# Projection stage: a third modulation group loaded earlier and multiplied inside the second step, and the decay constants moved to another pool

## The chip, the cores and the metric

The program runs on one core of a Trainium2 chip. The metric is the device time of one execution in microseconds (us), as the median of several runs; lower is better.

## The reference, cut to what matters

One layer of a diffusion backbone is applied to 128 context tokens and 512 latent tokens, together five tiles of 128 tokens, with 1024 channels. All is float32. The part that the change touches is the beginning: a modulated RMS norm, whose scale and shift come from a product of the conditioning vector with `w_mod`, and the projection of the result by `w_in`.

```
sh1, sc1, g1, sh2, sc2, g2 = adaln(c, w_mod[l], b_mod[l])       # silu(c) @ w_mod + b_mod, in six parts
h = rmsnorm(xs, norm1_g[l]) * (1.0 + sc1) + sh1
z = h @ w_in                                                    # q, k, v, rq, rk, rv, rg, ga, gr
...
lg_f = jax.nn.log_sigmoid(dec_f.astype(jnp.float32))            # retention: decay per head
q_decay = jnp.exp(lg * (i + 1.0))
k_decay = jnp.exp(lg * (CHUNK - 1.0 - i))
chunk_decay = jnp.exp(log_gamma * CHUNK)
```

The attention branch uses q, k, v; the retention branch uses rq, rk, rv, rg and the decays, which are functions of eight numbers for each direction. Both branches are projected, gated, added, and a gated MLP follows.

## The kernel before

TensorE multiplies in a fast 32-bit type, and each operand is split into a high part (a cast, by ScalarE) and a low part (the difference, by VectorE). One product of the reference thus becomes three matmuls (`mm3`, L158 to L161): high by high, high by low, low by high.

**The first stage** (from L426) is written out by hand, in the order of the instructions on TensorE, VectorE and ScalarE (`manual_schedule`). The tokens are normalised and transposed. Then eight steps follow, one for each block k of 128 channels. Step k, `z_kv(k)`, multiplies block k of all five token tiles by the 512 columns of `w_in` that make k and v, and adds into five PSUM banks `kvb` (mm1.mm.11 to mm1.mm.15). That is 15 matmuls a step. Before step k can start, four things must be there:

- `kv_hi` and `kv_lo` (L319, L324): high and low part of the weights of two steps, out of `weights.raw` (w_in, loaded at L313).
- `mod_mm(g)` (L386): products of the conditioning with the columns of `w_mod` for the channels of group g. The five groups hold 1, 1, 2, 2 and 2 blocks; their tiles are p0.u3 to p0.u7, each loaded by two transfers (L307), the scale's columns and the shift's. Group 2, p0.u5, serves the steps 2 and 3.
- `mod_row(g)` (L394) copies that product to SBUF, and `mod_vec(g)` (L400, a small matmul, then L402 and L404 on VectorE) turns it into vectors. `mod_vec` stands inside a step, after its second tile.
- `mod_hi(k)` (L409 on VectorE, L411 the cast on ScalarE) and `mod_lo(k)` (L414 on VectorE): block k modulated and split.

The loads are issued by SyncE's queue (SP) in the order of the lines from L327 on.

**The second stage** takes the five banks off: for each tile ScalarE copies k (L547) and casts v (L548) and squares k (L555), VectorE takes v's low part (L549) and sums (L556); tile 0 also has a copy (L552). Each bank is then reused: the q projection (`a_group`, five tiles with 12 matmuls for each half of the contraction) writes mm1.mm.16 into the bank of mm1.mm.11. GpSimd builds rotary tables meanwhile (L563, L566). From here on the program's order on each engine is set by a scheduler that places instructions by estimated times and by the buffers that they need; only the marked blocks keep the written order.

**The decay constants** (`decay_consts`, L576 to L599): 32 small operations on VectorE, on at most 16 numbers a row, and three on ScalarE, written after the attention and ahead of the attention's output projection. Their input `dec` and their scratch `dtmp` are tiles of the pool `const`, which is never reused, and so the scheduler could put the loads (L773, L774) and the chain much earlier than they are written. Their results `lg`, `lgsel`, `cdsel`, `kdec` are first used in the retention stage, after the output projection of the attention.

**The attention's output projection** (from L766) splits the attention's result (L645), multiplies it by `w_att_o` (L194 to L196, banks mm3.mm), and takes the banks off by L785 on VectorE; its pool `mod`, on the right side of SBUF, also holds the conditioning (`s128`) and one tile for `w_mod` (mod.wm, L248).

Of the kernel before, what the change touches and what calls it, by code (L numbers as in the profile page):

```python
# [69 lines left out]
def hybrid_step(ctx: ExitStack, tc: tile.TileContext, a: dict, o: dict):  # L70
# [40 lines left out]
    shvec = [cp([P, 8, 2]) for _ in range(2)]  # L111
    dec = cp([P, 2, 8])
    lg = cp([P, 2, 8])
    lgsel = cp([P, 8])
    cdsel = cp([P, 8])
    kdec = cp([P, 8, 2])
    dtmp = [cp([P, 2, 8]) for _ in range(3)]
    sso = cp([P, 2, NT, 4])
# [210 lines left out]
    kv_load(0, 2)  # L329
    mod_load(1)  # L330
    kv_load(2, 2)
    mod_load(2)
# [80 lines left out]
    def mod_lo(k):  # L413
        V.tensor_sub(hT[1][:, k, :], xnT[k // 4][:, k % 4], hT[0][:, k, :].bitcast(F32))  # L414
# [1174 lines left out]
```

## Time and profile before

| what | value |
|---|---|
| three runs | 1191.09, 1191.26 (median), 1192.38 us |
| the profiled execution | 1192.46 us, of which its span (first to last instruction) is 1190.7 us |
| mean granted TensorE clock | 0.994 |
| TensorE busy | 1156.5 us (97% of the span) |
| VectorE, ScalarE, GpSimd busy | 737.5, 567.4, 174.7 us |

All moments in this document are us from the start of the span. A row of the timeline gives the start, the duration, the engine, the line, the operation and the names "out<-in"; a bracket at its end tells how long the engine had been idle and who ended that. PE is TensorE, PEld its weight loads, DVE VectorE, ACT ScalarE, POOL GpSimd, SP SyncE, and a q behind a name is an engine's queue. Matmuls overlap: the next one starts before the one ahead has ended, so that the distance of the starts is what one costs. Lines are those of the kernel before; the changed kernel's stand one or two lower up to the attention and one higher after it.

### The profile page before, as it was taken

The page shows a single profiled execution, that of the slowest core. Times are in us where ns is not written, and L with a number is a line of the kernel's source. Part 1 is how long each engine was busy: PE and PEld are TensorE (multiplying, and loading weights), DVE is VectorE, ACT ScalarE, POOL GpSimd, SP SyncE. Part 2 cuts the span into 40 slices and gives each one's busy share as a digit, 9 for nine tenths or more (in the row PEclk, how much of TensorE's full clock was granted, in tenths as well). Part 3 has the DMA queues.
Part 4 walks back from the last instruction along what each step waited for, and adds up shares of the span by engine and source line. Part 5 has one row for each costly group of instructions (what it writes and reads, how often), then busy time and mean ns, then how long its engine had stood idle before and what let it go on. Part 6 is the DMA issues. An engine that isn't in the chain of part 4 may idle for free.

```text
span 1190.7 us, 18327 instructions
## 1 busy us (share of the span) xinstructions
PE 1156.5 (97%) x7317; PEld 1041.0 (87%) x7317; DVE 737.5 (62%) x1419; ACT 567.4 (48%) x1019; POOL 174.7 (15%) x177
## 2 busy tenths in 40 slices
PE   4999999999999999999999999999999999999996
PEld 3778899999988888778999988998989999899995
DVE  5576777754333526454323338968767687598887
ACT  4345655553132324443322335567657557475473
POOL 0032200000002200043011122011112111121113
PEclk9999999999999999999999999999999999999998
DMA  8831211016544522111122339536666658556553
GB/s 283 269 110 48 71 37 36 3 34 212 199 165 139 185 89 87 37 36 45 62 72 71 135 131 156 135 66 134 159 131 120 142 140 172 129 108 149 141 111 120
DMA packets 130917, 139.02 MB, mean 117 GB/s; under 512 B 26240, under 2 KB 98000, under 8 KB 130832
## 3 DMA queue, kind: packets, MB, share of 16 engines
q1 hardware_dynamic: 106592, 112.95, 29.3%
q0 software_dynamic: 24240, 24.91, 13.8%
q8 instruction: 57, 0.93, 0.3%
q14 instruction: 28, 0.23, 0.1%
HBM read 110.32 MB, written 6.03 MB: 98 GB/s over the span
## 4 chain that ended last, share of the span: by engine, by line
PE 89%; DVE 5%; SPq 1%; ACT 1%; DMA 1%; issue 1%; POOL 1%; DVEq 0%; POOLq 0%; ACTq 0%
DMA p0.u5.5_130<-in_w_mod 1%; SPq L313 0%; SPq L307 0%; POOL f0.s.5_3520 L940 0%; DVE acts.u2.2_101 L1104 0%; PE aux1.aux.6_337 L386 0%; DVE x1.u1.1_6376 L1076 0%; DVE acts.u1.1_100 L1103 0%; PE mm1.mm.16_720 L159 0%; PE mm7.mm.45_9650 L1383 0%; PE mm7.mm.9_7496 L1386 0%; PE mm7.mm.57_10402 L1383 0%; PE mm7.mm.33_8918 L1383 0%; PE mm7.mm.63_10768 L1385 0%; PE mm7.mm.54_10133 L1383 0%
## 5 line engine op out<-in xcount | busy, mean ns | idle before, releaser
L829 POOL TENSOR_TENSOR ret.r2k.6_3630<-ret.u5.5_3523,ret.u1.1_3516 128x256 f32<-128x256 f32 x2 | 1.4, 740 | 205.1 <-ACT ret.u5.5_3523 L825 205.1
L1397 DVE TENSOR_TENSOR t7.u4.4_6925<-t7.u4.4_6925,const.u1.1_70 128x322 f32<-128x322 f32 x10 | 5.0, 495 | 11.7 <-ACT const.u1.1_70 L1396 11.7
L878 DVE SCALAR_TENSOR_TENSOR ret2.u1.1_4317<-ret2.u1.1_4317,const.u14.14_94 64x128 f32<-64x128 f32 x24 | 6.8, 338 | 6.6 <-ACT ret2.u1.1_4317 L871 6.5
L411 ACT CAST acts.u1.1_100<-f0.s.1_113 128x640 fp32r<-128x640 f32 x4 | 2.9, 727 | 16.0 <-DVE f0.s.1_113 L409 16.0
L152 DVE TENSOR_TENSOR weights.wh.183_6565<-weights.raw.181_6562,weights.wh.182_6564 128x1024 fp32r<-128x1024 f32 x1 | 1.2, 1224 | 14.3 <-ACT weights.wh.182_6564 L147 14.3
L1308 POOL TENSOR_TENSOR x1.u1.1_6376<-x1.u1.1_6376,weights.raw.410_10987 128x512 f32<-128x512 f32 x5 | 8.2, 1637 | 10.4 <-ACT x1.tm.112_11000 L1280 7.5
L880 DVE SCALAR_TENSOR_TENSOR ret2.u1.1_4317<-ret2.u1.1_4317,const.u14.14_94 64x128 f32<-64x128 f32 x24 | 6.6, 383 | 4.8 <-ACT ret2.u1.1_4317 L873 4.8
L831 DVE TENSOR_TENSOR ret.u5.5_3523<-ret.u5.5_3523,ret.u1.1_3516 128x512 f32<-128x512 f32 x5 | 3.5, 692 | 9.4 <-POOL ret.r2k.8_3701 L829 3.3
L831 DVE TENSOR_TENSOR ret.u4.4_3522<-ret.u4.4_3522,ret.u1.1_3516 128x512 f32<-128x512 f32 x5 | 3.5, 692 | 9.0 <-POOL ret.r2k.11_3881 L829 4.7
L373 PE MATMUL mm1.mm.1_171<-const.u1.1_70,xin.u1.1_112 128*128 128x128 f32 x4 | 1.1, 432 | 7.1 <-DVE xin.u1.1_112 L364 7.1
L411 ACT CAST acts.u1.1_100<-f0.s.2_114 128x640 fp32r<-128x640 f32 x4 | 2.9, 727 | 10.6 <-DVE f0.s.2_114 L409 10.6
L563 POOL TENSOR_TENSOR p1.u1.1_613<-p1.u3.3_617,p1q.u1.1_607 128x512 f32<-128x512 f32 x1 | 1.4, 1428 | 43.2 <-DMA p1.u3.3_617<-in_rope 43.2
L152 DVE TENSOR_TENSOR weights.wh.108_4347<-weights.raw.106_4344,weights.wh.107_4346 128x1024 fp32r<-128x1024 f32 x1 | 1.2, 1225 | 10.3 <-ACT weights.wh.107_4346 L147 10.3
L147 ACT CAST weights.wh.112_4502<-weights.raw.111_4500 128x1024 fp32r<-128x1024 f32 x1 | 1.1, 1050 | 13.3 <-PE mm3.mm.36_4215 L160 13.3
L940 POOL TENSOR_TENSOR f0.s.5_3520<-f0.s.5_3520,ret2.ny20.11_4899 128x512 f32<-128x512 f32 x5 | 6.0, 1235 | 9.1 <-DVE ret2.ny20.11_4899 L219 9.1
L532 ACT ACTIVATE f0.s.3_719<-f0.s.3_719,p1q.ny20.11_887 128x128 f32<-128x128 f32 x20 | 6.0, 388 | 2.5 <-DVE p1q.ny20.11_887 L217 2.5
L373 PEld LDWEIGHTS mm1.mm.1_171<-const.u1.1_70,xin.u1.1_112 128*128 128x128 f32 x4 | 0.7, 216 | 7.3 <-DVE xin.u1.1_112 L364 7.3
L867 POOL DMA_DIRECT2D out_new_state_ret_fwd<-ret.r2k.25_4340 x1 | 0.7, 670 | 43.8 <-ACT ret.r2k.25_4340 L866 43.8
L259 DVE COPY mod2.wr.9_4307<-aux3.aux.15_4274 128x128 f32<-128x128 f32 x1 | 0.3, 291 | 10.9 <-PE aux3.aux.15_4274 L256 10.9
L1274 DVE TENSOR_TENSOR x1.u1.1_6376<-x1.u1.1_6376,gate.u1.1_5306 128x512 f32<-128x512 f32 x10 | 6.7, 681 | 0.0
L147 ACT CAST weights.wh.182_6564<-weights.raw.181_6562 128x1024 fp32r<-128x1024 f32 x1 | 1.1, 1055 | 11.5 <-PE mm3.mm.83_6396 L160 11.5
L147 ACT CAST weights.wh.67_3356<-weights.raw.66_3354 128x1024 fp32r<-128x1024 f32 x1 | 1.0, 1045 | 11.5 <-PE mm3.mm.8_3138 L195 11.5
(7028 smaller groups left out, 4884.6 us busy)
## 6 DMA issues: line engine op xcount, KB each, us to landing
spill.u1.1_6384<-x1.u1.1_6376 POOLq DMA_DIRECT2D x5, 512.0 KB, 4.2
xin.u1.1_112<-in_x_sample SPq DMA_DIRECT2D x4, 512.0 KB
p0.u5.5_130<-in_w_mod SPq DMA_DIRECT2D x2, 1024.0 KB
p0.u6.6_135<-in_w_mod SPq DMA_DIRECT2D x2, 1024.0 KB
p0.u7.7_138<-in_w_mod SPq DMA_DIRECT2D x2, 1024.0 KB
mod.wm.2_2916<-in_w_mod SPq DMA_DIRECT2D x1, 2048.0 KB
mod.wm.4_3067<-in_w_mod SPq DMA_DIRECT2D x1, 2048.0 KB
mod.wm.6_3222<-in_w_mod SPq DMA_DIRECT2D x1, 2048.0 KB
```

The lines of the kernel that those rows point to most:

```text
L147: nc.scalar.copy(hi, rv)
L152: (lo_eng or V).tensor_sub(lo, rv, hi.bitcast(F32))
L373: nc.tensor.transpose(xps[t, g][:, j * P:(j + 1) * P], xin[:, t, k * P:(k + 1) * P], ident)
L411: nc.scalar.copy(hT[0][:, k, :], xk)
L532: nc.scalar.activation(x[:, j], x[:, j], AF.Copy, scale=rstd[:, j:j + 1])
L831: V.tensor_mul(z, z, r1[:, t, 0:1, :].to_broadcast([P, 8, 64]))
L878: V.scalar_tensor_tensor(Ss[0:64, hh, st + 1, j], Ss[0:64, hh, st, j], cdsel[0:64, h:h + 1], Ss[0:64, hh, st + 1, j], op0=ALU.mult, op1=AL ...
L880: V.scalar_tensor_tensor(Ss[64:128, hh, 2 - st, j], Ss[64:128, hh, 3 - st, j], cdsel[64:128, h:h + 1], Ss[64:128, hh, 2 - st, j], op0=ALU. ...
L940: nc.gpsimd.tensor_mul(ov, ov, rso[:, 4 * t:4 * t + 4].unsqueeze(2).to_broadcast([P, 4, P]))
L1274: V.tensor_mul(x1[:, t, gs], x1[:, t, gs], gb[:, t == 0, gs])
L1308: eng.tensor_mul(x, x, fg[:, c0:c0 + 512])
L1397: V.tensor_sub(u[1][:, hi_u], u[1][:, hi_u], u3[i])
```

## The change

It has two parts that do not touch each other in the code.

1. `dec` and `dtmp` are no longer tiles of the pool `const` but of the pool `mod`, which is opened after the attention, on memory that the attention's buffers had.
2. In the first stage, the loads of group 2 of `w_mod` are issued ahead of the load of the weights of the steps 2 and 3. `mod_mm(2)`, with its `mod_row`, stands no longer ahead of step 1 but inside it, after its second tile, and `mod_vec(2)` after its third. `kv_lo(2)` stands behind `mod_hi(2)`, and `kv_lo(6)` behind `mod_lo(6)`, no longer ahead of `mod_mm(4)`.

```
-    dec = cp([P, 2, 8])
-    dtmp = [cp([P, 2, 8]) for _ in range(3)]
...
     mod_load(1)
+    mod_load(2)
     kv_load(2, 2)
-    mod_load(2)
...
-    def z_kv(k, mid=None):
+    def z_kv(k, mid=None, first=None):
         wh, wl = (x[:, (k % 2) * 512:(k % 2) * 512 + 512] for x in wkv[k - k % 2][1:])
         for t in range(NT):
             ts = slice(t * P, (t + 1) * P)
             mm3(kvb[t], hT[0][:, k, ts], hT[1][:, k, ts], wh, wl, k == 0, k == KD - 1)
-            if mid is not None and t == 1:
+            if first is not None and t == 1:
+                mod_mm(first)
+            if mid is not None and t == (1 if first is None else 2):
                 mod_vec(mid)
...
         kv_hi(2)
+        z_kv(1, 2, 2)
+        mod_hi(2)
         kv_lo(2)
-        mod_mm(2)
-        z_kv(1, 2)
-        mod_hi(2)
         mod_lo(2)
...
         kv_hi(6)
-        kv_lo(6)
         mod_mm(4)
         z_kv(4, 4)
         mod_hi(6)
         mod_lo(6)
+        kv_lo(6)
...
     mp = Pool("mod", side="right")
+    dec = mp([P, 2, 8])
+    dtmp = [mp([P, 2, 8]) for _ in range(3)]
     nc.sync.dma_start(dec[:, 0, :], a["decay_fwd"][0:1, :].to_broadcast([P, 8]))
     nc.sync.dma_start(dec[:, 1, :], a["decay_bwd"][0:1, :].to_broadcast([P, 8]))
-    decay_consts()
+    decay_consts(dec, dtmp)
```

The order of the instructions changes at these places. First SyncE's queue near the program's start, before the change, where p0.u4, p0.u5 and p0.u6 are the groups 1, 2 and 3 of `w_mod`, weights.raw.1 (its second half) the weights of the steps 2 and 3, and weights.raw.2 those of the steps 4 to 7:

```order
L307 DMA p0.u4.4_126<-in_w_mod 128x8x128 x2
L313 DMA weights.raw.1_124<-in_w_in 128x2x512
L307 DMA p0.u5.5_130<-in_w_mod 128x8x256 x2
L313 DMA weights.raw.2_133<-in_w_in 128x4x512
L307 DMA p0.u6.6_135<-in_w_mod 128x8x256 x2
```

And the same place after it:

```order
L305 DMA p0.u4.4_122<-in_w_mod 128x8x128 x2
L305 DMA p0.u5.5_125<-in_w_mod 128x8x256 x2
L311 DMA weights.raw.1_120<-in_w_in 128x2x512
L311 DMA weights.raw.2_129<-in_w_in 128x4x512
L305 DMA p0.u6.6_131<-in_w_mod 128x8x256 x2
```

The two transfers of group 2 (x2 in their row) went past one transfer of weights. On TensorE, at the end of step 0 and the beginning of step 1, before the change (the banks mm1.mm.11 to mm1.mm.15 are the five tiles of a step, aux1.aux.6 takes `mod_mm(2)`):

```order
L161 MATMUL mm1.mm.15_308<-weights.wh.3_241,acts.u2.2_101 128x512
L386 MATMUL aux1.aux.6_337<-p0.u5.5_130,p0.s128.8_146 32x128 x32
L159 MATMUL mm1.mm.11_304<-weights.wh.3_241,acts.u1.1_100 128x512
L160 MATMUL mm1.mm.11_304<-weights.wh.4_242,acts.u1.1_100 128x512
L161 MATMUL mm1.mm.11_304<-weights.wh.3_241,acts.u2.2_101 128x512
L159 MATMUL mm1.mm.12_305<-weights.wh.3_241,acts.u1.1_100 128x512
L160 MATMUL mm1.mm.12_305<-weights.wh.4_242,acts.u1.1_100 128x512
L161 MATMUL mm1.mm.12_305<-weights.wh.3_241,acts.u2.2_101 128x512
L400 MATMUL aux1.aux.7_378<-const.u1.1_70,p0.mrow.24_370 128x8
```

And after it:

```order
L159 MATMUL mm1.mm.15_304<-weights.wh.3_237,acts.u2.2_97 128x512
L157 MATMUL mm1.mm.11_300<-weights.wh.3_237,acts.u1.1_96 128x512
L158 MATMUL mm1.mm.11_300<-weights.wh.4_238,acts.u1.1_96 128x512
L159 MATMUL mm1.mm.11_300<-weights.wh.3_237,acts.u2.2_97 128x512
L157 MATMUL mm1.mm.12_301<-weights.wh.3_237,acts.u1.1_96 128x512
L158 MATMUL mm1.mm.12_301<-weights.wh.4_238,acts.u1.1_96 128x512
L159 MATMUL mm1.mm.12_301<-weights.wh.3_237,acts.u2.2_97 128x512
L384 MATMUL aux1.aux.6_338<-p0.u5.5_125,p0.s128.8_142 32x128 x32
L157 MATMUL mm1.mm.13_302<-weights.wh.3_237,acts.u1.1_96 128x512
L158 MATMUL mm1.mm.13_302<-weights.wh.4_238,acts.u1.1_96 128x512
L159 MATMUL mm1.mm.13_302<-weights.wh.3_237,acts.u2.2_97 128x512
L398 MATMUL aux1.aux.7_376<-const.u1.1_70,p0.mrow.24_371 128x8
```

The 32 products of group 2 now follow six matmuls of step 1 that they stood ahead of. On VectorE, at the steps 4 and 5, before the change (p0.mrow.26 is the row of group 4, weights.wh.10 the low part of the weights of the steps 6 and 7, and the first row is `mod_lo(5)`):

```order
L414 TENSOR_TENSOR acts.u2.2_101<-f0.s.2_114,acts.u1.1_100 128x640
L324 TENSOR_TENSOR weights.wh.10_481<-weights.raw.2_133,weights.wh.9_480 128x1024
L394 COPY p0.mrow.26_517<-aux1.aux.10_484 128x128
L402 TENSOR_TENSOR p0.u1.1_111<-aux1.aux.11_525,const.u3.3_83 128x2x4
L404 TENSOR_TENSOR p0.u1.1_111<-p0.u1.1_111,const.u3.3_83 128x4
```

And after it:

```order
L412 TENSOR_TENSOR acts.u2.2_97<-f0.s.2_110,acts.u1.1_96 128x640
L392 COPY p0.mrow.26_512<-aux1.aux.10_479 128x128
L400 TENSOR_TENSOR p0.u1.1_107<-aux1.aux.11_520,const.u3.3_83 128x2x4
L402 TENSOR_TENSOR p0.u1.1_107<-p0.u1.1_107,const.u3.3_83 128x4
L407 TENSOR_SCALAR f0.s.2_110<-f0.s.2_110,p0.u1.1_107 128x512
L407 TENSOR_SCALAR f0.s.2_110<-f0.s.2_110,p0.u1.1_107 128x128
L412 TENSOR_TENSOR acts.u2.2_97<-f0.s.2_110,acts.u1.1_96 128x640
L322 TENSOR_TENSOR weights.wh.10_477<-weights.raw.2_129,weights.wh.9_476 128x1024
```

The split of the weights went behind the row's copy and behind block 6. Last, VectorE where the banks are taken off, before the change (kv.u4 is v's low part, const.u16 and const.u18 the decays' scratch; ahead of these rows stand, since the split weights.wh.18, thirteen more operations of L581 to L588):

```order
L574 TENSOR_TENSOR kv.u4.4_603<-p1.vc.6_622,kv.u3.3_602 128x256
L587 TENSOR_TENSOR const.u16.16_96<-const.u16.16_96,const.u18.18_98 128x16
L588 TENSOR_SCALAR const.u16.16_96<-const.u16.16_96 128x16
L549 TENSOR_TENSOR kv.u4.4_603<-mm1.mm.11_304,kv.u3.3_602 128x256
L552 COPY p1.vt.7_627<-mm1.mm.11_304 128x256
```

And after it:

```order
L150 TENSOR_TENSOR weights.wh.15_728<-weights.raw.11_721,weights.wh.14_727 128x1024
L412 TENSOR_TENSOR acts.u2.2_97<-f0.s.2_110,acts.u1.1_96 128x640
L150 TENSOR_TENSOR weights.wh.18_794<-weights.raw.16_791,weights.wh.17_793 128x1024
L548 TENSOR_TENSOR kv.u4.4_599<-mm1.mm.11_300,kv.u3.3_598 128x256
L551 COPY p1.vt.7_623<-mm1.mm.11_300 128x256
```

No operation of the decays stands between the split of the weights and the banks any more. All of `decay_consts` now stands on VectorE in the attention's output projection: the first operation (L578), which waits for the load of `dec`, behind the third of the eight splits L645, the others among the first four L785. On SyncE the two loads of `dec` stand ahead of the first load of mod.wm, and they wait for three instructions near the attention's end: the transposition into aux2.aux.50 (TensorE), and L699 (ScalarE) and L702 (VectorE) of the last context block. Of the other 6115 rows of TensorE only some at the beginning of the output projection change places among themselves.

More of the change, by code (lines that the diff above doesn't have):

```diff
@@ L111, in hybrid_step @@
     shvec = [cp([P, 8, 2]) for _ in range(2)]
-    dec = cp([P, 2, 8])
     lg = cp([P, 2, 8])
@@ L116, in hybrid_step @@
     kdec = cp([P, 8, 2])
-    dtmp = [cp([P, 2, 8]) for _ in range(3)]
     sso = cp([P, 2, NT, 4])
@@ L330, in hybrid_step @@
     mod_load(1)
+    mod_load(2)
     kv_load(2, 2)
-    mod_load(2)
     kv_load(4, 4)
@@ L414, in mod_lo, with z_kv @@
         V.tensor_sub(hT[1][:, k, :], xnT[k // 4][:, k % 4], hT[0][:, k, :].bitcast(F32))
-    def z_kv(k, mid=None):
+    def z_kv(k, mid=None, first=None):
         wh, wl = (x[:, (k % 2) * 512:(k % 2) * 512 + 512] for x in wkv[k - k % 2][1:])
@@ L420, in z_kv @@
             mm3(kvb[t], hT[0][:, k, ts], hT[1][:, k, ts], wh, wl, k == 0, k == KD - 1)
-            if mid is not None and t == 1:
+            if first is not None and t == 1:
+                mod_mm(first)
+            if mid is not None and t == (1 if first is None else 2):
                 mod_vec(mid)
@@ L478, in hybrid_step @@
         kv_hi(2)
+        z_kv(1, 2, 2)
+        mod_hi(2)
         kv_lo(2)
-        mod_mm(2)
-        z_kv(1, 2)
-        mod_hi(2)
         mod_lo(2)
@@ L495, in hybrid_step @@
         kv_hi(6)
-        kv_lo(6)
         mod_mm(4)
@@ L500, in hybrid_step @@
         mod_lo(6)
+        kv_lo(6)
         mod_hi(7)
@@ L574, in hybrid_step, with decay_consts @@
     V.tensor_sub(vv[1][:, 5, :], vc.rearrange("p h d -> p (h d)"), vv[0][:, 5, :].bitcast(F32))
-    def decay_consts():
+    def decay_consts(dec, dtmp):
         e, s, s2 = dtmp
@@ L772, in hybrid_step @@
     mp = Pool("mod", side="right")
+    dec = mp([P, 2, 8])
+    dtmp = [mp([P, 2, 8]) for _ in range(3)]
     nc.sync.dma_start(dec[:, 0, :], a["decay_fwd"][0:1, :].to_broadcast([P, 8]))
     nc.sync.dma_start(dec[:, 1, :], a["decay_bwd"][0:1, :].to_broadcast([P, 8]))
-    decay_consts()
+    decay_consts(dec, dtmp)
     ada = mod_rest((("sc", 1, 4096), ("sh", 1, 3072)), mp, aux)
```

## The prediction

> **What bounds the kernel now.** I read the totals first, then who waited for whom, then windows of 2 us, then the timeline of the first 75 us.
>
> ```profile
> PE 1156.5 (97%) x7317; PEld 1041.0 (87%) x7317; DVE 737.5 (62%) x1419; ACT 567.4 (48%) x1019; POOL 174.7 (15%) x177
> ...
> PE mm1.mm.16_720 L159 <- DVE p1.vt.7_627 L552: 2.9, 1, 2.9
> PE aux1.aux.6_337 L386 <- DMA p0.u5.5_130<-in_w_mod: 2.3, 1, 2.3
> PE aux1.aux.11_525 L400 <- DVE p0.mrow.26_517 L394: 1.1, 1, 1.1
> ```
>
> TensorE is the bound: 97% busy, with few waits. Three of these (who waited, for whom, total, times, longest) lie where the change works. TensorE also slows after the longer ones. A row of the windows gives the stretch, its length, the busy time (and instructions) of PE, PEld, DVE, ACT and POOL, then the granted clock PEclk, the DMA share and GB/s:
>
> ```profile
> 28.00:30.00 2.00, 0.27 (x4) 0.00 (x0) 2.00 (x3) 0.67 (x1) 0.00 (x0) 1.00 1.07 372
> 30.00:32.00 2.00, 1.43 (x28) 1.34 (x32) 0.32 (x1) 0.00 (x0) 0.00 (x0) 0.61 1.05 377
> 32.00:34.00 2.00, 2.00 (x40) 1.59 (x32) 0.00 (x0) 0.00 (x0) 0.00 (x0) 0.53 1.09 348
> ...
> 50.00:52.00 2.00, 1.28 (x6) 0.71 (x4) 1.87 (x2) 1.85 (x2) 0.00 (x0) 1.00 0.00 0
> ...
> 68.00:70.00 2.00, 1.69 (x4) 1.43 (x5) 2.00 (x7) 1.41 (x6) 0.93 (x1) 0.50 0.03 10
> ```
>
> Behind the waits of 2.3 and 2.9 us the clock is near half; at the wait of 1.1 us, which begins at 51.3, it is 1.00. So each long wait is paid twice.
>
> **Term 1: group 2 inside step 1.** On TensorE, and on the engines that feed step 2:
>
> ```profile
> 27.53 0.40 PE L161 MATMUL mm1.mm.15_308<-weights.wh.3_241,acts.u2.2_101 128*128 128x512 f32 x1
> ...
> 28.50 0.68 DVE L324 TENSOR_TENSOR weights.wh.4_242<-weights.raw.1_124,weights.wh.3_241 128x512 fp32r<-128x512 f32 x1
> ...
> 29.10 1.22 DVE L324 TENSOR_TENSOR weights.wh.6_334<-weights.raw.1_124,weights.wh.5_333 128x1024 fp32r<-128x1024 f32 x1
> ...
> 30.57 3.53 PE L386 MATMUL aux1.aux.6_337<-p0.u5.5_130,p0.s128.8_146 128*32 128x128 f32 x60 [2.30 <-DMA p0.u5.5_130<-in_w_mod]
> ...
> 35.52 0.28 PE L400 MATMUL aux1.aux.7_378<-const.u1.1_70,p0.mrow.24_370 128*128 128x8 f32 x2
> ...
> 36.25 0.80 DVE L409 TENSOR_SCALAR f0.s.1_113<-f0.s.1_113,p0.u1.1_111 128x512 f32<-128x512 f32 x2
> ...
> 37.84 0.83 DVE L414 TENSOR_TENSOR acts.u2.2_101<-f0.s.1_113,acts.u1.1_100 128x640 fp32r<-128x640 f32 x1 [0.79 <-ACT acts.u1.1_100 L411]
> ...
> 38.72 0.50 PE L161 MATMUL mm1.mm.11_304<-weights.wh.5_333,acts.u2.2_101 128*128 128x512 f32 x1
> ...
> 41.95 1.95 PE L386 MATMUL aux1.aux.8_418<-p0.u6.6_135,p0.s128.8_146 128*32 128x128 f32 x64
> ```
>
> After the change step 1 begins at 27.8. Its second matmul needs the low weights of L324, done at 28.50 + 0.68 = 29.2. The other five of two tiles start 0.23 apart (rows 64.77 and 65.00 below) and are through at 30.4, the pause before them being 1.1 us. Group 2 is there by then: it landed at 30.57 behind 0.5 MB more, and at the 372 GB/s of the window 28 to 30 that is 1.4 us, so at about 29.2; were it no earlier, 0.2 us would be lost. At full clock its 64 records take the 1.95 us of row 41.95, to 32.35. One tile more, 0.8 us, brings L400 to 33.15, against 35.52.
>
> Before, L161 of step 2 came 3.20 us behind L400 (38.72 − 35.52). Now VectorE also does `kv_lo(2)`, 1.22 us, between L409 and L414, where it had idled 0.79 us: 0.43 more. L161 starts at 33.15 + 3.2 + 0.4 = 36.75, **2.0 us earlier**. The cast `kv_hi(2)` waits for weights that now land last, at about 30.6; ScalarE does nothing then and is needed for step 2 only near 34.7.
>
> What is late next: groups 3 and 4, whose bytes ahead are unchanged. They began at 41.95 and 47.73 without a wait, and are now wanted at 39.9 and 45.7. Behind the landing at 30.57 come, by their shapes, 1.05 MB of weights and 2.1 MB of group 3; at the 348 to 377 GB/s of the windows 30 to 34 that is 8.4 to 9.0 us, so 39.0 to 39.6, and group 4, 2.1 MB more, 44.6 to 45.6. Both are covered, but only by some tenths.
>
> **Term 2: the row of group 4.**
>
> ```profile
> 47.73 1.95 PE L386 MATMUL aux1.aux.10_484<-p0.u7.7_138,p0.s128.8_146 128*32 128x128 f32 x64
> ...
> 49.98 0.83 DVE L414 TENSOR_TENSOR acts.u2.2_101<-f0.s.2_114,acts.u1.1_100 128x640 fp32r<-128x640 f32 x1 [0.79 <-ACT acts.u1.1_100 L411]
> ...
> 50.94 1.23 DVE L324 TENSOR_TENSOR weights.wh.10_481<-weights.raw.2_133,weights.wh.9_480 128x1024 fp32r<-128x1024 f32 x1
> ...
> 52.08 0.28 DVE L394 COPY p0.mrow.26_517<-aux1.aux.10_484 128x128 f32<-128x128 f32 x1
> ...
> 52.42 0.39 PE L400 MATMUL aux1.aux.11_525<-const.u1.1_70,p0.mrow.26_517 128*128 128x8 f32 x2 [1.14 <-DVE p0.mrow.26_517 L394]
> ```
>
> TensorE waited 1.14 us for the copy L394, which stood behind the split of 1.23 us. Without that split the copy follows L414: 50.81 − 2.0 + 0.28 = 49.1. TensorE arrives at 45.7 + 1.95 + six matmuls of 0.23 = 49.05. L400 at 49.15 instead of 52.42 is 3.27 earlier, **1.3 us** beyond term 1. The split now ends near 53.5 and is wanted by step 6 at 55: covered.
>
> **Term 3: the banks.**
>
> ```profile
> 52.19 0.38 SPq L136 DMA_DIRECT2D weights.raw.16_795<-in_w_in  x1
> ...
> 60.49 1.28 DVE L581 TENSOR_SCALAR const.u17.17_97<-const.u16.16_96 128x16 f32<-128x16 f32 x1
> ...
> 58.27 1.05 ACT L147 CAST weights.wh.17_797<-weights.raw.16_795 128x1024 fp32r<-128x1024 f32 x1 [0.80 <-PE mm1.mm.15_308 L160]
> ...
> 62.93 0.38 ACT L548 CAST kv.u3.3_602<-mm1.mm.11_304 128x256 fp32r<-128x256 f32 x1
> ...
> 64.77 0.40 PE L160 MATMUL mm1.mm.15_308<-weights.wh.10_481,acts.u1.1_100 128*128 128x512 f32 x1
> ...
> 65.00 0.40 PE L161 MATMUL mm1.mm.15_308<-weights.wh.9_480,acts.u2.2_101 128*128 128x512 f32 x1
> ...
> 66.61 0.17 DVE L588 TENSOR_SCALAR const.u16.16_96<-const.u16.16_96 128x16 f32<-128x16 f32 x1
> ...
> 67.42 0.42 DVE L549 TENSOR_TENSOR kv.u4.4_603<-mm1.mm.11_304,kv.u3.3_602 128x256 fp32r<-128x256 f32 x1
> ...
> 67.75 0.41 DVE L552 COPY p1.vt.7_627<-mm1.mm.11_304 128x256 f32<-128x256 f32 x1
> ...
> 68.31 0.77 PE L159 MATMUL mm1.mm.16_720<-weights.wh.12_727,acts.u1.1_100 128*128 128x512 f32 x1 [2.91 <-DVE p1.vt.7_627 L552]
> ...
> 72.58 0.39 PE L159 MATMUL mm1.mm.17_721<-weights.wh.12_727,acts.u1.1_100 128*128 128x512 f32 x1
> ```
>
> And the transfers of the half microsecond from 57.0:
>
> ```profile
> 57.00:57.50 0.50, 0.50 (x4) 0.42 (x3) 0.50 (x1) 0.47 (x1) 0.00 (x0) 1.00 0.32 30
> ```
>
> The cast that L549 needs is done at 63.3, but VectorE works on the decays from 60.49 to 67.4. Without them the bank is free when two other chains are through. TensorE ends step 7 at 65.23 − 3.3 = 61.95. The load raw.16, issued at 52.19 when L324 had freed its buffer, now goes at 53.5. Its data were in by 57, where only 30 GB/s still flow, at most 4.8 us behind the issue, hence 58.3 now. Its cast (1.05, row 58.27) and split (1.22, as in row 29.10) stand ahead of the bank's: 60.6, then 0.4 + 0.4 gives 61.4, a margin of 0.6. So TensorE goes on at 61.95: the gap of 3.08 (65.23 to 68.31) is gone, **3.1 us**. And the twelve matmuls of the first tile take 12 × 0.23 + 0.1 = 2.9 instead of 4.27 (68.31 to 72.58): **1.4 us**.
>
> **Term 4: the decays' new place.** In the output projection TensorE has no slack but VectorE has much:
>
> ```profile
> 254.88 0.59 ACT L644 CAST att.pT0.195_2676<-aux2.aux.50_2671 128x512 fp32r<-128x512 f32 x1 [1.44 <-PE aux2.aux.50_2671 L658]
> ...
> 268.71 0.37 SPq L248 DMA_DIRECT2D mod.wm.2_2916<-in_w_mod  x1
> ...
> 270.61 3.04 DVE L645 TENSOR_TENSOR ya.u2.2_2833<-f0.s.3_719,ya.u1.1_2832 128x640 fp32r<-128x640 f32 x4
> ...
> 268.00:338.00 70.00, 70.00 (x672) 67.77 (x671) 27.07 (x47) 16.47 (x22) 0.00 (x0) 1.00 0.55 187
> ```
>
> The 32 operations, 0.17 us each (row 66.61) and with the step to the next about 0.2, or 6.5 us, go into 43 us of idle VectorE; five banks rotate there, and a bank taken off 1 us later stops nobody. The loads of `dec` wait for aux2.aux.50, used at 254.88, and are needed behind three L645, at 272.9: 18 us. I take 0, with bounds of −0.1 (rows change places) and +0.4.
>
> **The sum.** 2.0 + 1.3 + 3.1 + 1.4 = 7.8 us; behind it everything is TensorE's and only moves. Against the profiled execution, 1192.46, that gives 1184.7; it is 1.2 above the median of 1191.26, from which it gives 1183.5. Whether those 1.2 us come from the stretches at half clock, which go, I cannot tell: I take the middle, **1184.1**.
>
> **The rivals.**
>
> *The margins do not hold* (groups 3 and 4, or raw.16, land later than my sums of bytes). For it: the margins are 0.3 to 0.9 us. Against it: a miss costs only what goes beyond them. If group 3 is no earlier than 41.95, term 1 is lost, and 1186.1 remains; a wait of 1 to 2 us for raw.16 gives 1185.1 to 1186.1. Chance 0.18.
>
> *The clock falls all the same*, in the pauses of 1.1 us at 28 and together about 1.2 us before 36.75. Price as in the rows: 3.53 − 1.95 = 1.6, or 1.4, so about 1185.7. The wait of 1.14 speaks against it. Chance 0.10.
>
> *The slow stretches do not belong to these waits.* Then 1.6 of term 1 and the 1.4 stay, and the gain is 4.8: 1187.1. For it: three rows alone cannot show a rule. Against it: both follow a wait at once. Chance 0.05. By the Trainium skill, "TensorE: Matmul & The Clock Gate", section "What's actually happening", the clock is halved only after at least one idle window of about 3.4 us; by that rule neither wait could have halved it and this rival's time would come out, but the trace has it halved after 2.30 us.
>
> *The decays' load comes late* and L578 holds the splits L645 behind it, for which TensorE waits. If the load went only beside mod.wm at 268.71 and took as long as group 2 in its queue (row below), 11.73 us, it would land at 280.4: 7.5 us of stall and 1.4 of half clock, 8.9, more than the 7.8 gained: 1193.0, 1.7 us slower than the median now. It decides from a stall of about 5.8 us, a landing at 278.7. The order of the queue and the 18 us of slack speak against it. Chance 0.04.
>
> ```profile
> 18.79 11.73 DMA p0.u5.5_130<-in_w_mod
> ```
>
> *The gains are given back later*, at a place where TensorE waits for something that does not move with it; no such wait over 1.3 us follows in the list of waits. 1191.3. Chance 0.03.
>
> **The numbers.** Forecast 0.60, the rivals 0.18, 0.10, 0.05, 0.04 and 0.03. The range reaches down to the sum from the median less some tenths for the bounds (1182.8) and up to the slow stretches that stay (1187.2); what it leaves out is the last two rivals and the tails. 0.2%, about what a measurement can tell from no change here, is 2.4 us. The first four cases are faster by more; of the last two I put 0.04 within and 0.03, a stall over 8.5 us or its like, slower: 0.93, 0.04, 0.03.
>
> **What would show it.** Right: no wait for p0.u5; PEclk 1.00 from 28 to 75; L161 of step 2 near 36.7; L400 of group 4 near 49.1; mm1.mm.16 near 62, mm1.mm.17 near 64.8; the output projection as long as before. Wrong: a wait of TensorE for p0.u6, p0.u7 or L552; a clock under 1 before 75; a gap at L645.

## The result, and the profile after

The changed kernel takes **1184.86 us** (median of 4 runs, 1184.57 to 1185.04) against 1191.82 (median of 4, 1191.09 to 1192.38) for the kernel before on the same chip: a ratio of 0.9942, 95% interval 0.9924 to 0.9959. That is 7.0 us; forecast were 1184.1, with 1182.8 to 1187.2 as the range. In the profiled executions the span falls from 1190.7 to 1182.9, by 7.8, which was the sum. First the page's line of busy times, with TensorE's share one point up:

```profile
PE 1153.6 (98%) x7317; PEld 1038.8 (88%) x7317; DVE 738.3 (62%) x1419; ACT 567.1 (48%) x1019; POOL 175.9 (15%) x177
```

The list of TensorE's waits no longer has the three that the prediction named. What is left near the change are the rows for step 0 and step 2 (together, L157) and for the low weights in step 1 (L158):

```profile
PE mm1.mm.11_300 L157 <- ACT acts.u1.1_96 L409: 1.3, 2, 0.8
PE mm7.mm.12_7686 L1384 <- ACT t7.u1.1_6922 L1389: 1.3, 1, 1.3
PE mm1.mm.11_300 L158 <- DVE weights.wh.4_238 L322: 1.0, 1, 1.0
```

The windows that stood at 0.61, 0.53 and 0.50 have the full clock (the column behind the five engines):

```profile
28.00:30.00 2.00, 1.04 (x4) 0.67 (x4) 1.42 (x2) 0.00 (x0) 0.00 (x0) 1.00 1.05 388
30.00:32.00 2.00, 2.00 (x48) 1.55 (x50) 0.00 (x0) 1.05 (x1) 0.00 (x0) 1.00 1.05 374
32.00:34.00 2.00, 2.00 (x38) 1.63 (x28) 0.46 (x2) 0.00 (x0) 0.00 (x0) 1.00 1.09 349
...
68.00:70.00 2.00, 2.00 (x10) 1.66 (x9) 1.97 (x4) 0.00 (x0) 2.00 (x4) 1.00 0.90 243
```

And the timeline at the places of the terms: the rows answer to those of before one by one (29.48 and 30.83 to the wait for group 2, 36.96 to 38.72, 49.35 to 52.42, 62.13 to 68.31, 65.00 to 72.58).

```profile
29.48 0.50 PE L158 MATMUL mm1.mm.11_300<-weights.wh.4_238,acts.u1.1_96 128*128 128x512 f32 x1 [0.95 <-DVE weights.wh.4_238 L322]
...
30.83 1.96 PE L384 MATMUL aux1.aux.6_338<-p0.u5.5_125,p0.s128.8_142 128*32 128x128 f32 x64
...
33.52 0.28 PE L398 MATMUL aux1.aux.7_376<-const.u1.1_70,p0.mrow.24_371 128*128 128x8 f32 x2
...
36.96 0.50 PE L159 MATMUL mm1.mm.11_300<-weights.wh.5_329,acts.u2.2_97 128*128 128x512 f32 x1 [0.23 <-DVE acts.u2.2_97 L412]
...
49.35 0.33 PE L398 MATMUL aux1.aux.11_520<-const.u1.1_70,p0.mrow.26_512 128*128 128x8 f32 x2
...
53.74 0.37 SPq L134 DMA_DIRECT2D weights.raw.16_791<-in_w_in  x1
...
59.01 1.05 ACT L145 CAST weights.wh.17_793<-weights.raw.16_791 128x1024 fp32r<-128x1024 f32 x1 [3.86 <-DMA weights.raw.16_791<-in_w_in]
...
60.09 1.23 DVE L150 TENSOR_TENSOR weights.wh.18_794<-weights.raw.16_791,weights.wh.17_793 128x1024 fp32r<-128x1024 f32 x1 [2.71 <-ACT weights.wh.17_793 L145]
...
61.57 0.41 DVE L551 COPY p1.vt.7_623<-mm1.mm.11_300 128x256 f32<-128x256 f32 x1
...
62.13 0.48 PE L157 MATMUL mm1.mm.16_716<-weights.wh.12_723,acts.u1.1_96 128*128 128x512 f32 x1
...
65.00 0.39 PE L157 MATMUL mm1.mm.17_717<-weights.wh.12_723,acts.u1.1_96 128*128 128x512 f32 x1
...
247.26 0.34 SPq L774 DMA_DIRECT2D mod.u1.1_2849<-in_decay_fwd  x1
...
265.22 0.17 DVE L577 TENSOR_SCALAR mod.u2.2_2850<-mod.u1.1_2849 128x16 f32<-128x16 f32 x1
```

mm1.mm.17 is 7.58 us earlier; behind it next to nothing changes. In all fourteen profiles of this study the rest of the span, from mm1.mm.17 on, is 1117.7 to 1118.1 us, so the start of that matmul sums up what a kernel did to the first stage, to some tenths:

| kernel | median us (runs) | kernel before in the same runs | mm1.mm.17 starts |
|---|---|---|---|
| before | | | 72.58 |
| changed | 1184.86 (4) | 1191.82 | 65.00 |
| decays alone | 1187.68 (5) | 1192.07 | 68.12 |
| group 2 alone | 1185.47 (5) | 1192.07 | 65.93 |
| old load order | 1185.04 (5) | 1192.07 | 65.19 |
| split 6 early | 1186.46 (5) | 1192.07 | 66.36 |
| before, tables held | 1187.44 (5) | 1191.38 | 67.95 |
| products ahead | 1183.92 (5), again 1184.15 (5) | 1191.38, 1191.12 | 64.42, 64.12 |
| three attempts beyond | 1185.36 (5), 1183.99 (5), 1184.21 (6) | 1191.38, 1191.48, 1191.12 | 65.87, 64.38, 64.39 |
| one more split, two more | 1186.63, 1188.70 (1 each) | 1191.48, 1191.38 | 66.84, 69.00 |

The first attempt had a sixth run, of 1517.21 us at a mean clock of 0.703, which is not in its median.

### The profile page after: what moved, and what is told of

Its sections match the earlier page's. It is cut to its first block, busy times and chain, and to the rows that moved or that the text cites. A ratio compares the mean times of both kernels' runs of the same rounds, so it can differ in the third digit from the quotient of the medians.

```text
span 1182.9 us, 18329 instructions
## 1 busy us (share of the span) xinstructions
PE 1153.6 (98%) x7317; PEld 1038.8 (88%) x7317; DVE 738.3 (62%) x1419; ACT 567.1 (48%) x1019; POOL 175.9 (15%) x177
## 3 DMA queue, kind: packets, MB, share of 16 engines
q1 hardware_dynamic: 106592, 112.95, 29.4%
## 4 chain that ended last, share of the span: by engine, by line
PE 88%; DVE 4%; issue 3%; DMA 2%; POOL 1%; ACT 1%; SPq 0%; DVEq 0%; POOLq 0%; ACTq 0%
DMA t7.u5.5_6930<-in_conv_w 1%; POOL x1.u1.1_6376 L1077 1%; POOL f0.s.5_3520 L941 0%; DVE acts.u2.2_97 L1105 0%; DMA xin.u1.1_108<-in_x_sample 0%; DMA x1.u1.1_6376<-in_x_prompt 0%; DVE acts.u1.1_96 L1104 0%; DVE acts.u2.2_97 L412 0%; PE mm1.mm.11_300 L159 0%; PE mm7.mm.9_7496 L1387 0%; PE mm7.mm.45_9650 L1384 0%; PE mm7.mm.33_8918 L1384 0%; PE mm7.mm.57_10402 L1384 0%; PE mm7.mm.54_10133 L1384 0%; PE mm7.mm.42_9401 L1384 0%
## 5 line engine op out<-in xcount | busy, mean ns | idle before, releaser
L879 DVE SCALAR_TENSOR_TENSOR ret2.u1.1_4317<-ret2.u1.1_4317,const.u13.13_93 64x128 f32<-64x128 f32 x24 | 6.8, 339 | 6.6 <-ACT ret2.u1.1_4317 L872 6.5
L881 DVE SCALAR_TENSOR_TENSOR ret2.u1.1_4317<-ret2.u1.1_4317,const.u13.13_93 64x128 f32<-64x128 f32 x24 | 6.6, 383 | 4.8 <-ACT ret2.u1.1_4317 L874 4.8
```

Source lines behind the costliest of these rows:

```text
L879: V.scalar_tensor_tensor(Ss[0:64, hh, st + 1, j], Ss[0:64, hh, st, j], cdsel[0:64, h:h + 1], Ss[0:64, hh, st + 1, j], op0=ALU.mult, op1=AL ...
L881: V.scalar_tensor_tensor(Ss[64:128, hh, 2 - st, j], Ss[64:128, hh, 3 - st, j], cdsel[64:128, h:h + 1], Ss[64:128, hh, 2 - st, j], op0=ALU. ...
```

## Experiments: which part carries the gain

**The decays alone.** The kernel before with the first part of the change.

```
-    dec = cp([P, 2, 8])
-    dtmp = [cp([P, 2, 8]) for _ in range(3)]
...
     mp = Pool("mod", side="right")
+    dec = mp([P, 2, 8])
+    dtmp = [mp([P, 2, 8]) for _ in range(3)]
```

> The kernel before with the decay constants alone in the projection stage's pool; loads, products of group 2 and the split of group 6's weights as before. By the prediction's sum this is worth terms 3's 3.1 + 1.4 us: 4.5 us below the kernel before, about 1187.3; no wait at the first matmul of mm1.mm.16, the clock 1.00 from 60 to 76 us, but the wait of 2.3 us for group 2 and the half clock behind it at 30 to 34 us still there. Rival: the two parts need each other, and with group 4's products still 3.3 us late something else holds the bank; then under 3 us are won.

Measured: 4.4 us below the kernel before (ratio 0.996, 0.9948 to 0.9973). The windows of this kernel show what it mends and what not:

```profile
32.00:34.00 2.00, 2.00 (x33) 1.59 (x26) 0.20 (x1) 0.00 (x0) 0.00 (x0) 0.50 1.09 349
...
68.00:70.00 2.00, 2.00 (x11) 1.62 (x10) 1.86 (x8) 0.09 (x1) 0.00 (x0) 1.00 0.21 66
```

The wait for group 2 (2.1 us) and the half clock behind it stay, the gap at 65 and its half clock are gone. The 3.1 and 1.4 us of term 3 have their size: mm1.mm.17 is 4.5 earlier.

**Group 2 alone.** The changed kernel with `dec` and `dtmp` back in `const`, the same lines the other way round.

> The changed kernel with the decay constants back in the kernel-wide pool, so that their 32 operations stand in the first stages again. If the parts add up, this wins terms 1 and 2 alone, 2.0 + 1.3 = 3.3 us below the kernel before, about 1188.3, and mm1.mm.16 still waits about 3 us for L552 (here L553), with half clock behind it. Rival: in this order of VectorE the first 14 decay operations stand ahead of the split of raw.16, where VectorE idled 2.7 us in the changed kernel (57.4 to 60.1); they would end at 60.3 to 61.3, the bank would come free at 62.1 to 63.2 against 62.1 wanted, and this kernel would be only 0 to 1.1 us slower than the changed one: 6 to 7 us below the kernel before, and the move of the decays worth almost nothing by itself.

Measured: 6.6 us below the kernel before (0.9945, 0.9933 to 0.9958), where 3.3 would be the sum of its terms. The rival holds. Its timeline, with 14 decay operations between the first and the second row:

```profile
58.13 0.17 DVE L582 TENSOR_SCALAR const.u17.17_97<-const.u16.16_96 128x16 f32<-128x16 f32 x1
...
60.92 0.18 DVE L588 TENSOR_TENSOR const.u16.16_96<-const.u16.16_96,const.u18.18_98 128x16 f32<-128x16 f32 x1
61.02 1.23 DVE L152 TENSOR_TENSOR weights.wh.18_798<-weights.raw.16_795,weights.wh.17_797 128x1024 fp32r<-128x1024 f32 x1
...
62.50 0.41 DVE L553 COPY p1.vt.7_627<-mm1.mm.11_304 128x256 f32<-128x256 f32 x1
...
63.06 0.48 PE L159 MATMUL mm1.mm.16_720<-weights.wh.12_727,acts.u1.1_100 128*128 128x512 f32 x1
63.23 1.31 POOL L564 TENSOR_TENSOR p1.u1.1_613<-p1.u3.3_617,p1q.u1.1_607 128x512 f32<-128x512 f32 x1 [46.03 <-PE mm1.mm.15_308 L161]
```

The scheduler now puts the decays into the time in which VectorE has nothing to do but wait for raw.16, and the bank is free at 62.91, 0.1 us late. The parts do not add up: 4.4 + 6.6 = 11.0 against 7.0 together. The gap before mm1.mm.16 goes by either part, and with the second in place the first is worth next to nothing: mm1.mm.17 is 0.93 later here than in the changed kernel, and 0.80 of that stood already ahead of step 0, which neither part touches (its first matmul is at 24.59 here, at 23.79 there).

What differs from the kernel before is not only where the 14 operations stand but how long they take: here 0.21 us each from start to start, with GpSimd idle. Before, 15 of them and the low part of the cached v (0.42) filled 60.49 to 67.4, with GpSimd's rotary tables beside them:

```profile
60.31 1.43 POOL L563 TENSOR_TENSOR p1.u1.1_613<-p1.u3.3_617,p1q.u1.1_607 128x512 f32<-128x512 f32 x1 [43.25 <-DMA p1.u3.3_617<-in_rope]
...
63.39 1.29 POOL L563 TENSOR_TENSOR p1q.u2.2_608<-p1.u3.3_617,p1q.u1.1_607 128x512 f32<-128x512 f32 x1
63.49 1.22 DVE L588 TENSOR_SCALAR const.u16.16_96<-const.u16.16_96 128x16 f32<-128x16 f32 x1
...
64.63 1.70 POOL L566 TENSOR_TENSOR p1q.u3.3_609<-p1.u3.3_617,p1q.u1.1_607 128x128 f32<-128x128 f32 x4
...
64.75 0.39 DVE L587 TENSOR_TENSOR const.u16.16_96<-const.u16.16_96,const.u18.18_98 128x16 f32<-128x16 f32 x1
```

Eleven decay operations start while GpSimd's products run (60.31 to 66.34). Two of them, L582 and L583, take as long as alone. Each of the nine others ends 0.03 or 0.04 us after one of GpSimd's products has ended: L581 (60.49 and 1.28 us) at 61.77 behind 61.74, L588 at 64.71 behind 64.68. So they were held until a product was through.

**The kernel before, tables held.** Nothing of the change; GpSimd's order is fixed there, so that its tables stand behind the store of `vt`, which waits for L552.

```
+    with tc.manual_schedule(engines={ET.Pool}):
-    for t in range(NT):
+        for t in range(NT):
...
-    for i in (1, 0):
+        for i in (1, 0):
```

> The kernel before, its decays where they were and VectorE's order row for row the same; only GpSimd's ten rope-table products (60.31 to 66.3) are held until the copy L552 has freed the bank, by a fixed order on its queue. Theory: it was the company of GpSimd that made the decays hold the bank. 14 operations in the second kernel's trace stood 0.21 apart with GpSimd idle and took 2.9 us; in the kernel before they and one split took 6.9. Alone they end at about 63.7, the bank is free at about 64.9 against 65.23 wanted: no gap, no half clock, 4 to 4.5 us below the kernel before, as much as moving the decays brings. Rival: the number of decay operations is what holds the bank; then at least 2 us of the gap stay, half clock behind them, and the gain is under 1.5 us.

Measured: 3.9 us below the kernel before (0.9961, 0.9949 to 0.9973). VectorE's rows and GpSimd's first product:

```profile
60.43 0.17 DVE L582 TENSOR_SCALAR const.u17.17_97<-const.u16.16_96 128x16 f32<-128x16 f32 x1
...
63.02 0.17 DVE L589 TENSOR_SCALAR const.u16.16_96<-const.u16.16_96 128x16 f32<-128x16 f32 x1
...
64.16 0.41 DVE L552 COPY p1.vt.7_629<-mm1.mm.11_304 128x256 f32<-128x256 f32 x1
...
65.17 0.39 PE L159 MATMUL mm1.mm.16_723<-weights.wh.12_730,acts.u1.1_100 128*128 128x512 f32 x1
...
65.82 1.33 POOL L564 TENSOR_TENSOR p1.u1.1_613<-p1.u3.3_617,p1q.u1.1_607 128x512 f32<-128x512 f32 x1
```

Up to the banks the same operations, in the same order, end 3.6 us earlier (L552 starts at 64.16, before at 67.75), TensorE has no gap there and the clock stays at 1.00 from 60 to 72. So the decays held the bank only in GpSimd's company. By the Trainium skill, "SBUF — State Buffer", section "SBUF: two separate sides", some VectorE operations and GpSimd share a pair of ports that one holds for its whole instruction while the other blocks; the rows agree, with 0.17 us alone and 0.32 to 1.28 for those nine operations, which end with GpSimd's products.

**The old load order.** The changed kernel with its loads as before.

```
     mod_load(1)
-    mod_load(2)
     kv_load(2, 2)
+    mod_load(2)
```

> The changed kernel with the loads in their old order (group 2 behind the second pair of weights). By the prediction group 2 then lands at 30.6, as before, and its products want it at 30.8: no wait, 0 to 0.2 us slower than the changed kernel. Rival: the order of the loads carries the gain, since in the changed kernel the products begin without a wait only because of it; then TensorE waits for p0.u5 by over 0.5 us and the time is 1 us or more above the changed kernel.

Measured: 1185.04, level with the changed kernel. The wait of step 1 and the products of group 2:

```profile
29.73 0.50 PE L158 MATMUL mm1.mm.11_300<-weights.wh.4_238,acts.u1.1_96 128*128 128x512 f32 x1 [0.96 <-DVE weights.wh.4_238 L322]
...
31.09 1.96 PE L384 MATMUL aux1.aux.6_338<-p0.u5.5_126,p0.s128.8_142 128*32 128x128 f32 x64
```

No wait at the products: once they stand inside step 1, the order of the loads is worth 0.2 us at most.

**The products ahead of step 1**, with the new load order.

```
-        z_kv(1, 2, 2)
+        mod_mm(2)
+        z_kv(1, 2)
```

> The changed kernel with its loads, but the products of group 2 ahead of step 1, as before. By the prediction group 2 lands at about 29.2: TensorE waits about 1.2 us from 28.0 at full clock, the low weights at 29.4 are hidden behind it, and step 2 begins 0.5 to 1.0 us earlier than in the changed kernel, if groups 3 and 4 land in time; the time is 0 to 0.9 us below the changed kernel. Rival: the loads do not bring group 2 forward (landing at 30.5 as before), then the wait of over 2 us and the half clock are back and the time is 1.5 to 2 us above the changed kernel: then the placement inside step 1 carries term 1.

Measured in two sets of runs: 1183.92 (1183.75 to 1184.09) and 1184.15 (1183.87 to 1184.32), 7.5 and 7.0 us below the kernel before in the same runs (0.9935, 0.9923 to 0.9947; 0.9938, 0.9926 to 0.995). The second of the two profiles, for which step 0 began early:

```profile
29.21 1.94 PE L384 MATMUL aux1.aux.6_332<-p0.u5.5_125,p0.s128.8_142 128*32 128x128 f32 x60 [1.06 <-DMA p0.u5.5_125<-in_w_mod]
...
31.42 0.40 PE L158 MATMUL mm1.mm.11_300<-weights.wh.4_238,acts.u1.1_96 128*128 128x512 f32 x1
...
36.03 0.50 PE L159 MATMUL mm1.mm.11_300<-weights.wh.5_329,acts.u2.2_97 128*128 128x512 f32 x1 [0.24 <-DVE acts.u2.2_97 L412]
```

Group 2 is there at 29.2, as forecast (in the first profile, whose step 0 began 0.9 later, at 29.4, after a wait of 0.34). The wait of 1.06 us replaces the 0.95 for the low weights, which are split meanwhile, and the selection matmul comes one tile earlier in step 1: step 2 is through its wait at 36.03 instead of 36.96. Its spans are 1182.1 both times, against 1182.9, and its runs do not overlap those of the changed kernel; but the two were never timed in the same set, and the changed kernel's ratio to the kernel before, 0.9942 (0.9924 to 0.9959), lies within the intervals of the two above, so that the 0.7 to 0.9 us between them rest on the profiles. Either edit by itself does away with the half clock: the products alone remove the wait for group 2, the loads alone shorten it and cover the low weights with what is left, which by the profiles is the better of the two.

**Split 6 early.** The changed kernel with one row of VectorE moved back.

```
         kv_hi(6)
+        kv_lo(6)
...
-        kv_lo(6)
```

> The changed kernel with one row of VectorE moved back: the split of the weights of steps 6 and 7 stands ahead of the copy of group 4's row again. By the prediction (term 2) the copy ends 1.2 us later, TensorE waits about 1.1 us at the selection matmul of group 4 (at 49.35 in the changed kernel), at full clock, and the time is 1.1 to 1.3 us above the changed kernel. Rival: it is absorbed by a later wait (the bank at 62 or the weights of step 6), and under 0.4 us remain.

Measured: 1186.46, 1.6 above the changed kernel; mm1.mm.17 is 1.36 later. The wait is back in its old size:

```profile
50.77 0.39 PE L398 MATMUL aux1.aux.11_521<-const.u1.1_70,p0.mrow.26_513 128*128 128x8 f32 x2 [1.14 <-DVE p0.mrow.26_513 L392]
```

## Experiments: the clock

The prediction had three waits to go by: the clock halved behind 2.30 and 2.91 us and not behind 1.14. Two kernels lengthen the wait of step 1, and nothing else, by doing the split that TensorE waits for once or twice more.

```
         kv_lo(0, 1)
+        kv_lo(0, 1)
```

> The changed kernel with the split that TensorE waits for in step 1 done three times instead of once, 0.61 us apart: the wait of 0.95 us becomes about 2.2 us, nothing else moves. If half clock follows a wait of somewhere between 1.14 and 2.30 us, as the rows of before suggest, the products of group 2 (64 records, 1.96 us) take up to 3.5 us and the time is 2.5 to 2.8 us above the changed kernel. If the clock has nothing to do with such a wait, or needs one over 3 us, the products take 1.96 us and only 1.2 us are lost.

Measured: 1188.70 (one run), 3.8 above the changed kernel, of which 1.5 is wait. Behind it the matmuls stand 0.43 apart, and the products take nearly twice as long:

```profile
30.65 0.80 PE L158 MATMUL mm1.mm.11_300<-weights.wh.4_238,acts.u1.1_96 128*128 128x512 f32 x1 [2.41 <-DVE weights.wh.4_238 L322]
...
33.08 3.64 PE L384 MATMUL aux1.aux.6_340<-p0.u5.5_125,p0.s128.8_142 128*32 128x128 f32 x64
```

More was lost than expected, because the clock stayed down twice as long: in narrow windows it is at half from 30.16 to 36.99, 6.83 us, against 3.41 (30.45 to 33.86) and 3.41 (68.00 to 71.41) in the kernel before.

> The changed kernel with the split that TensorE waits for in step 1 done twice: by the last experiment's 0.7 us for each further split the wait becomes about 1.65 us. The clock stood at 1.00 behind waits of up to 1.17 us in these traces and fell to half behind 2.1 us and more. If it falls here too, the products of group 2 take over 2.5 us and the matmuls behind the wait stand 0.4 us apart; if the limit lies above 1.65, they take 1.96 us and stand 0.23 apart, and the time is 0.7 us above the changed kernel.

Measured: 1186.63 (one run), 1.8 above the changed kernel, of which 0.7 is wait. The row of the wait, a matmul behind it, the products, and a row of the windows:

```profile
29.79 0.50 PE L158 MATMUL mm1.mm.11_300<-weights.wh.4_238,acts.u1.1_96 128*128 128x512 f32 x1 [1.68 <-DVE weights.wh.4_238 L322]
...
30.83 0.63 PE L158 MATMUL mm1.mm.12_301<-weights.wh.4_238,acts.u1.1_96 128*128 128x512 f32 x1
...
31.81 2.85 PE L384 MATMUL aux1.aux.6_339<-p0.u5.5_125,p0.s128.8_142 128*32 128x128 f32 x64
```

```profile
30.00:32.00 2.00, 2.00 (x9) 1.12 (x12) 0.00 (x0) 1.04 (x1) 0.00 (x0) 0.57 1.05 375
```

A wait of 1.68 us was enough here, and the clock is down for 3.41 us (30.30 to 33.71) again. The longest that left the clock at 1.00 in this stage is 1.17 (step 0 of the kernel with the products ahead).

The length of the wait is not the whole condition. In every profile the moments at which the clock changes lie whole multiples of 3.413 us apart (30.45 and 68.00 in the kernel before: eleven), wherever the waits are, and the second stretch of before begins 0.31 us ahead of the end of its wait. So it looks as if the clock is set at the ends of windows of that length, by TensorE's idle time inside each. Ahead of the half clock this is 2.18 and 2.59 us in the kernel before (27.04 to 30.45, 64.58 to 68.00), 2.07 with the decays alone, 2.21 with the tables held, 1.92 with two more splits and 1.68 with one more. In the other windows from 20 to 76 us that begin at full clock it is at most 1.29. The limit is not sharp: near the program's end windows with up to 1.80 us of idle time are followed by full clock.

A window at half clock with at most 0.32 us of idle time is followed by full clock; the first one of the kernel with two more splits, with 0.49, is followed by another at half. By this a wait of some 2 us that the end of a window cuts in two could leave the clock alone; no profile here has one.

## Experiments: attempts at more

**The first**, from the changed kernel: the splits of steps 1 and 2 earlier, the products of group 4 inside step 4, the second half of the weights behind group 3.

```
-    kv_load(4, 4)
+    kv_load(4, 2)
     mod_load(3)
+    kv_load(6, 2)
...
+        kv_lo(0, 1)
         kvb = [mm([P, 512], tag="mm") for _ in range(NT)]
         z_kv(0, 1)
...
-        kv_lo(0, 1)
         kv_hi(2)
+        kv_lo(2)
         z_kv(1, 2, 2)
         mod_hi(2)
-        kv_lo(2)
...
-        mod_mm(4)
-        z_kv(4, 4)
+        z_kv(4, 4, 4)
```

> An attempt at a faster kernel, from the changed one: the two low-weight splits that TensorE or VectorE's chain wait for in steps 1 and 2 stand earlier on VectorE (one ahead of step 0, one ahead of the copy of group 2's row), the products of group 4 stand inside step 4, and the second half of the weights' load stands behind the load of group 3. It removes the pause of 0.95 us in step 1 and about 0.4 us of VectorE ahead of step 2: 1.0 to 1.4 us below the changed kernel, about 1183.7. Rival: the transfers are the bound there, groups 2, 3 and 4 land when they did, TensorE waits for one of them instead, and 0.3 us or less is won.

Measured: 1185.36, no gain but 0.5 above the changed kernel. The front did move (the pause in step 1 is gone), but group 4's vectors came later, with them the split of the weights of step 6, behind which raw.16 can be loaded, and TensorE waits for the bank:

```profile
53.30 1.22 DVE L322 TENSOR_TENSOR weights.wh.10_478<-weights.raw.2_129,weights.wh.9_477 128x1024 fp32r<-128x1024 f32 x1
...
63.00 0.48 PE L157 MATMUL mm1.mm.16_717<-weights.wh.12_724,acts.u1.1_96 128*128 128x512 f32 x1 [0.59 <-ACT p1.u4.4_616 L546]
```

**The second and the third** start from the kernel with the products ahead, load like the first, and split earlier for steps 2 and 6. The second has group 4's products inside step 4, as in this diff; the third has them ahead of it.

```
         mod_mm(2)
+        kv_lo(2)
         z_kv(1, 2)
         mod_hi(2)
-        kv_lo(2)
...
-        mod_mm(4)
-        z_kv(4, 4)
+        z_kv(4, 4, 4)
         mod_hi(6)
+        kv_lo(6)
         mod_lo(6)
-        kv_lo(6)
```

> From the kernel with the products of group 2 ahead of step 1: the split for step 2 stands ahead of VectorE's work on group 2's vectors, the products of group 4 stand inside step 4, the second half of the weights' load stands behind group 3, and the split for step 6 stands between the scaling of column 6 and its low part, so that the load of raw.16 goes out about 1.5 us earlier than it did. The wait of 0.23 us and about 0.2 us of VectorE's chain at step 2 go, and the front moves by as much if groups 3 and 4 are there: 0.4 to 0.8 us below that kernel's 1183.9, so 1183.1 to 1183.5. Rival: groups 3 or 4, or the bank at 61, hold TensorE again, as the bank did for 0.6 us in the first attempt: no gain, or some tenths lost.

> The kernel of the last attempt with the products of group 4 ahead of step 4 again. There the third matmul of step 4 stood 0.53 us behind its second instead of 0.23, since the low part of column 4 was not ready and no products lay ahead of it to cover that. With the products ahead this 0.3 us goes, and what the earlier split for step 2 won (0.3 us from step 0 to group 3's products) stays: 0.3 us below 1184.0, about 1183.7. Rival: group 4 has not landed at 44.9; TensorE waits for it instead, and nothing is won.

> The kernel with the products of group 2 ahead of step 1 once more, as it stands, beside the last attempt on the same chip, since the two differ by some tenths only: 1183.9, 0.3 us above the last attempt if its theory holds, level with it if the rival does.

Measured: 1183.99 and 1184.21, level with the 1183.92 and 1184.15 of the kernel that they start from. Each wins 0.25 us by group 3's products (from group 2's on: 9.78 us against 10.02 and 10.03) and loses as much at step 4. Inside the step, the products no longer cover the wait for the low part of column 4: its third matmul, 45.77, stands 0.53 behind the second. Ahead of it, in the third attempt, they are held by the transfers: 2.37 us where the same 64 records take 1.95 in the second.

```profile
45.10 2.37 PE L385 MATMUL aux1.aux.10_480<-p0.u7.7_135,p0.s128.8_143 128*32 128x128 f32 x64
```

From here on the transfers bound the first stage as much as the order of the instructions: where the products of group 4 are held (by 0.2 us at 45.34 in the first profile with the products ahead, by 0.4 at 45.10 here), both put its landing at about 45.5, by estimate; in the second profile with the products ahead, at 45.14, they are held by 0.1.

## Why the prediction was right, and where its reasons were not

- **Term 1** (2.0 forecast): step 2's row at 36.96 instead of 38.72, 1.8 us. The missing 0.2 is the start of step 1, 28.01 instead of 27.8. Group 2 at 29.2 is right, but in the changed kernel nobody needs it so early: the old load order gives the same time. That term put the gain down to both edits, and either would have done.
- **Term 2** (1.3): 52.42 − 49.35 is 3.07, 1.3 beyond term 1. Undone by itself, the edit costs 1.4 to 1.6.
- **Term 3** (3.1): 68.31 − 62.13 is 6.18, 3.1 beyond the others. The size is right, and the cause was half of it. The step that was incomplete is "VectorE works on the decays from 60.49 to 67.4. Without them the bank is free": the same decays, in the same place, leave the bank free in time when GpSimd stands still, and in an idle stretch of VectorE too. The quoted rows held the hint: 0.17 us for one operation and 1.28 for another of the same size. The terms were added as if each part had its own; the two single parts win 4.4 and 6.6. That the sum holds all the same is partly luck: the prediction counted this gap once, for the decays, and did not see that the second part closes it without them.
- **The margin of raw.16** (0.6): 0.1. The load took 5.27 us from issue to cast where 4.8 was the bound, the bank was free at 61.98 and wanted at 62.09. The rival of the margins came that near; the first attempt above shows its price.
- **The clock** (1.4, and 1.6 inside term 1): 72.58 − 65.00 is 7.58, 1.4 beyond the rest, and no window of the stage is under 1.00. The rival that the clock falls all the same counted on pauses of 1.1 and 1.2 us; they were 0.95, and 0.56 and 0.23. The rival that the slow stretches belong to something else is refuted by the two kernels with longer waits. By the Trainium skill, "TensorE: Matmul & The Clock Gate", section "What's actually happening", the gate works in windows of about 3.4 us and halves the clock after an idle one. The length agrees with the stretches of 3.41 us and one of twice that; the condition does not, since 1.68 us of idle time in a window were enough.
- **The decays' new place** (0): their loads go out at 247.3, the first operation starts at 265.22 without a wait, and TensorE is busy for 70.00 of the 70 us of the output projection. The rival with a late load did not come about; a kernel with a late load was not tried.
- **The 1.2 us** between the profiled execution and the median of before: unexplained then. The runs of the kernels that keep a stretch at half clock (before, decays alone, tables held) lie 1.3 to 4.9 us apart, those of the changed kernel and of the ones without such a stretch (group 2 alone, old load order, split 6 early, products ahead, the attempts) 0.2 to 0.9. The runs of the decays alone fall into two groups, 1186.2 to 1186.3 and 1187.7 to 1187.9, and those of the tables held likewise, 1186.0 to 1186.2 and 1187.4 to 1187.8; the steps are about what one stretch costs. That goes with a stretch that comes in one execution and not in another, as it could where the waits fall differently into the windows, but all profiled executions of these kernels have their stretches, so it is not shown.

## What to carry to other kernels

Before a busy engine is blamed for holding a buffer, compare its operations' durations with the same ones elsewhere: where they are longer, look at what runs beside them. Here the company was the cause, and moving either party helped. Gains of two edits that end at the same wait are not to be added; price each with the other in place. Work that does not hang on a chain belongs where TensorE would wait for that chain, ahead of it, provided that its own data are there (here, by the profiles, 0.7 to 0.9 us).

## What the runs showed of the hardware

- The granted clock fell to half behind a TensorE wait of 1.68, 2.1, 2.3, 2.4 and 2.9 us, and not behind 0.95 to 1.17. It changes at moments that lie multiples of 3.413 us apart, and stayed at half for 3.41 us, once for 6.83; ahead of it a window of that length had 1.68 us or more of idle time. By the times of the single runs the added wait of 0.7 us cost 1.0 us beyond itself and that of 1.5 cost 2.4; from the first matmul of step 0, which began 0.4 and 0.3 us earlier in these two than in the changed kernel, to mm1.mm.17 it is 1.5 and 2.8.
- An operation of VectorE on 16 numbers a row takes 0.17 us alone, and in the kernel before nine of the eleven beside GpSimd's products took 0.32 to 1.28, each until one of those products had ended. In the kernel with group 2 alone, one on 10 numbers a row took 3.59 us, from 66.12 to 69.71, while GpSimd did six products, from 66.30 to 69.67:

```profile
66.12 3.59 DVE L207 TENSOR_SCALAR p1.nm10.13_667<-p1.ssk.5_620 128x10 f32<-128x10 f32 x1
```
